# A hybrid decoder layer on one core: the delta rule's output with value channels on partitions, and the inverse's last levels paired across all heads

## The chip, the core and the metric

The kernel runs on one core of a Trainium2 chip. The core has five engines with queues of their own: TensorE (PE; its weight loads are listed as PEld), VectorE (DVE), ScalarE (ACT), GpSimd (POOL), and SyncE (SP), which here only issues DMAs. The metric is the device time of one execution in microseconds; the kernel before takes 1123.69 us (median of 3 runs, 1123.31 to 1124.84).

## The reference

One layer on 1024 tokens of width 1024 in float32. After an RMSNorm with shift and scale, one projection feeds two groups side by side: a gated linear recurrence (RG-LRU, 512 channels) and a gated delta rule (4 heads of width 128). Their normalized outputs go through one output projection; a squared-ReLU MLP of width 4096 and a final RMSNorm follow. The change lies in the delta rule, computed in chunks, and in the normalization of its output:

```python
u = triangular_solve(tmat, v_beta);  w = triangular_solve(tmat, k_beta * exp(g))
attn = where(causal, einsum('bhnid,bhnjd->bhnij', q, k) * decay, 0.0)
...
def step(state, inp):
    v_new = u_n - einsum('bhck,bhkv->bhcv', w_n, state)
    o = einsum('bhck,bhkv->bhcv', qd_n, state) + einsum('bhij,bhjv->bhiv', attn_n, v_new)
    state = state * gl_n[..., None, None] + einsum('bhck,bhcv->bhkv', kt_n, v_new)
    return state, o
...
out_gdn = rms_norm(o, gdn_norm_w) * silu(z)          # per head and token
mix = concatenate([out_lru, out_gdn], axis=-1) @ w_out
```

q and k are normalized to unit length per head and token. A scale of q passes through o, so the kernel never scales q: it adds the sum of squares of q, with its factors, to the epsilon of o's norm.

## The kernel before

All matrices are held as tiles of 128 partitions by 1024 columns in a pool of 46 (`big`), with PSUM tiles of 512 columns (`ps`) and DRAM tiles for what must wait long (`z_d`, `k_d`, `dm_d`, `cat_d`). The large products (input projections, output projection, MLP) split each f32 operand into a high and a low f32r part and take three f32r products (`mm3`). The smaller ones, in the delta rule, are plain f32, which the profile shows as two PE instructions each; a transpose is one.

The program is first recorded as a list of operations (`Recorder`), each with its predecessors. It is then emitted in an order that stands in the file as packed data: `ORDER` is one permutation of all operations of all engines, and `SLOTS` gives each tile its buffer. Each engine and the DMA queue run their part of it in this order. All loads and nearly all stores go through SP's queue.

Because every operation is recorded by one helper, almost all rows of the profile show line 319; operations are told apart by the names of their tiles. `mms` records several matmuls as one operation (line 445).

The delta rule uses chunks of 128 tokens, 8 per head:

- `key(h)`: the convolved key `k_`, its transposes `ktok`, the products `kk`, and the matrices `LT` of all 32 chunks.
- `inverse()`: inverts the 32 unit triangular matrices. DVE inverts the 32x32 diagonal blocks of all chunks at once. Then PE joins them: `it` and `iy` join 32 to 64, `iw` and `iz` join 64 to 128. `iw(h)` reads partitions 0 to 63 and writes 64 to 127, `iz(h)` the other way round. ACT takes `iw` out of PSUM (`after_iw`) and `iz` reads the result; DVE takes `iz` out (`after_iz`). `mixed` alternates the matmuls of two blocks.
- `query(h)`: the convolved q with channels on partitions, its 8 transposes `qtok` for the sums of squares (`ssqq`), and the products `qk` with keys, multiplied by the decay (tile `dm`).
- `value(h)`: the values, transposed (`vtok`) to tokens on partitions (tile `nv`).
- `chain(h)`: the recurrence over the 8 chunks. Per chunk the products with the state and the inverse are `ch`, the output's two products `cho`:

```python
mm(po[:, os4], qT[:, ts_], S, True, False)
mm(po[:, os4], dm[:, ts_], vn, S is None, True)
```

The first operand after the output is the stationary one; the result has its columns on partitions. So o comes out with tokens on partitions. After the last chunk, o is squared (`zt`), summed over each row (`rso`), scaled by the inverse root (POOL's power, `rsqrt8`), transposed back with 8 PE transposes (`oT`), multiplied by the gate z (`zz`) and stored to `cat_d`, from where the output projection loads it (`gcm`, split into `gch` and `gcl`).

PE fills the gaps of the recurrence with the input projections (`q_p`, `v_p`, `lx_p`, `ly_p`). The output projection (`wg`, `wl`) and the MLP (`up...`, `dn`) follow. `mod_row` computes a row of factors, stores it to DRAM (`modd`) and loads it broadcast to all partitions (`g_bc`); its sum over partitions is a block of four matmuls into 32 partitions each (`g_r`).

## Time and profile before

| | |
|---|---|
| runs | 1123.31, 1123.69, 1124.84 us |
| span of the profiled execution, first to last instruction | 1121.3 us |
| busy: PE, PEld | 1111.5, 934.3 us |
| busy: DVE, ACT, POOL | 795.0, 622.0, 254.0 us |
| granted TensorE clock, mean | 0.998 |
| DMA | 234.00 MB, 209 GB/s on average |

The page gives of the profiled execution its span alone; the median of the runs is 2.4 us longer. In the rows, a group reads: line, engine, operation, out<-in by tile names, shape, count, then busy time and the mean length of one instruction. In the timeline, a row is start, length, engine, line, operation, and how many of one kind in sequence it stands for. PE's instructions overlap, so lengths add up to more than the time.

### The profile page before, as it was taken

The page shows a single profiled execution, that of the slowest core. Times are in us where ns is not written, and L with a number is a line of the kernel's source. Part 1 is how long each engine was busy: PE and PEld are TensorE (multiplying, and loading weights), DVE is VectorE, ACT ScalarE, POOL GpSimd, SP SyncE. Part 2 cuts the span into 40 slices and gives each one's busy share as a digit, 9 for nine tenths or more (in the row PEclk, how much of TensorE's full clock was granted, in tenths as well). Part 3 has the DMA queues.
Part 4 walks back from the last instruction along what each step waited for, and adds up shares of the span by engine and source line. Part 5 has one row for each costly group of instructions (what it writes and reads, how often), then busy time and mean ns, then how long its engine had stood idle before and what let it go on. Part 6 is the DMA issues. An engine that isn't in the chain of part 4 may idle for free.

```text
span 1121.3 us, 16537 instructions
## 1 busy us (share of the span) xinstructions
PE 1111.5 (99%) x6282; PEld 934.3 (83%) x6282; DVE 795.0 (71%) x1122; ACT 622.0 (55%) x967; POOL 254.0 (23%) x159
## 2 busy tenths in 40 slices
PE   9999999999999999999999999999999999999997
PEld 8889889999988877888888888788888888888886
DVE  4859886877878796888675767768664583874573
ACT  6549644466488973786555545556555333453352
POOL 1000100101011442100113123132400366903030
PEclk9999999999999999999999999999999999999999
DMA  9808716567632354321777586778999757954511
GB/s 348 257 20 293 252 38 184 162 195 244 209 96 95 114 206 128 135 85 58 262 239 285 189 277 234 257 243 310 401 397 396 257 183 256 335 173 179 206 75 75
DMA packets 127688, 234.00 MB, mean 209 GB/s; under 512 B 10933, under 2 KB 51450, under 8 KB 127610
## 3 DMA queue, kind: packets, MB, share of 16 engines
q1 hardware_dynamic: 127370, 232.73, 59.8%
q8 instruction: 49, 0.80, 0.3%
q10 hardware_dynamic: 240, 0.23, 0.1%
q14 instruction: 29, 0.24, 0.1%
HBM read 174.18 MB, written 58.74 MB: 208 GB/s over the span
## 4 chain that ended last, share of the span: by engine, by line
PE 93%; ACT 2%; DVE 1%; DMA 1%; issue 1%; SPq 1%; POOL 0%; POOLq 0%; ACTq 0%; DVEq 0%
PE dn L319 27%; PE upx L319 16%; PE upz L319 8%; PE q_p L319 4%; PE k_p L319 4%; PE v_p L319 4%; PE wg L319 4%; PE upy L319 4%; PE ly_p L319 4%; PE lx_p L319 4%; PE wl L319 3%; PE z_p L319 3%; PE ch L319 2%; PE cho L319 1%; DMA wk<-in_w_in_dram 1%
## 5 line engine op out<-in xcount | busy, mean ns | idle before, releaser
L319 PE MATMUL upx<-h2h,U 128*128 128x512 f32 x512 | 167.9, 395 | 0.0
L319 PEld LDWEIGHTS upx<-h2h,U 128*128 128x128 f32 x512 | 96.2, 188 | 22.5
L319 ACT ACTIVATE act<-act 128x512 f32<-128x512 f32 x112 | 70.8, 632 | 58.6 <-DVE act L319 56.5
L319 PE MATMUL upx<-h2l,U 128*128 128x512 f32 x256 | 101.1, 395 | 0.0
L319 POOL TENSOR_TENSOR wd<-wd,wd 128x512 f32<-128x512 f32 x32 | 46.4, 1452 | 236.2 <-DMA wd<-in_w_down_dram 143.5
L319 DVE TENSOR_TENSOR U<-wu,U 128x512 fp32r<-128x512 f32 x112 | 84.4, 776 | 20.7 <-ACT U L319 19.7
L319 PE MATMUL upz<-h2h,U 128*128 128x512 f32 x256 | 85.0, 394 | 0.0
L319 ACT CAST U<-wu 128x512 fp32r<-128x512 f32 x112 | 65.4, 617 | 19.9 <-DVE wu L319 18.2
L319 PEld LDWEIGHTS upx<-h2l,U 128*128 128x128 f32 x256 | 48.1, 188 | 11.8 <-issue 0.4
L319 PEld LDWEIGHTS upz<-h2h,U 128*128 128x128 f32 x256 | 48.1, 188 | 11.1
L319 ACT COPY ek<-upx 128x512 f32<-128x512 f32 x48 | 28.0, 583 | 51.3 <-PE upx L319 50.8
L319 PE MATMUL upz<-h2l,U 128*128 128x512 f32 x128 | 50.3, 393 | 0.0
L319 DVE TENSOR_TENSOR act<-upz,ek 128x512 f32<-128x512 f32 x32 | 22.1, 690 | 36.7 <-ACT ek L319 17.9
L319 POOL TENSOR_TENSOR R<-R,R_5o 128x1024 f32<-128x1024 f32 x8 | 24.5, 3077 | 80.6 <-DMA L<-aod 69.9
L319 PE MATMUL upy<-h2h,U 128*128 128x512 f32 x128 | 42.7, 395 | 0.0
L319 DVE TENSOR_TENSOR wu<-wu,wu 128x512 f32<-128x512 f32 x48 | 36.0, 760 | 2.1 <-DMA wu<-in_w_up_dram 1.9
L319 ACT ACT_TABLE_LOAD x24 | 30.8, 1283 | 2.5 <-issue 2.1
L319 POOL TENSOR_TENSOR ssq<-ssq,mhalf 128x1 f32<-128x1 f32 x16 | 12.8, 805 | 81.1 <-DVE ssq L319 81.0
L319 PE MATMUL q_p<-hh,q_wh 128*128 128x256 f32 (+2 forms) x96 | 30.1, 339 | 0.0
L319 PE MATMUL v_p<-hh,v_wh 128*128 128x256 f32 (+2 forms) x96 | 29.8, 340 | 0.0
L319 PE MATMUL q_p<-hl,q_wh 128*128 128x512 f32 (+2 forms) x96 | 29.7, 336 | 0.0
L319 PE MATMUL lx_p<-hh,lx_wh 128*128 128x256 f32 (+2 forms) x96 | 29.6, 333 | 0.0
(576 smaller groups left out, 3468.4 us busy)
## 6 DMA issues: line engine op xcount, KB each, us to landing
L<-aod SPq DMA_DIRECT2D x56, 512.0 KB, 5.1
R<-in_w_down_dram SPq DMA_DIRECT2D x40, 512.0 KB, 7.2
wu<-in_w_up_dram SPq DMA_DIRECT2D x32, 512.0 KB, 4.5
aod<-as SPq DMA_DIRECT2D x64, 256.0 KB, 5.6
wd<-in_w_down_dram SPq DMA_DIRECT2D x32, 512.0 KB, 5.2
aod<-act SPq DMA_DIRECT2D x48, 256.0 KB, 2.7
x<-in_x_dram SPq DMA_DIRECT2D x16, 512.0 KB, 3.6
sc_w<-in_w_mod_dram SPq DMA_DIRECT2D x16, 512.0 KB, 7.9
```

The lines of the kernel that those rows point to most:

```text
L319: op.fn(*[res(v) for v in op.a], **{n: res(v) for n, v in op.k.items()})
```

## The change

- `chain`: the output's products swap their operands, so that o comes out with value channels on partitions, which is the layout of z. Each half of o is squared out of PSUM by ACT (over `nv`, now called `os_`) and multiplied by z by DVE. The load of z moves ahead of the recurrence.
- `query`: the transposes `qtok` and the sums over their squares go. ACT squares q whole (`qs`).
- The norm: `os_ + qs` is summed over partitions by a block of four matmuls with `ones`, 32 output partitions each (`on{h}`). DVE turns 32x32 blocks so that the 1024 sums stand on partitions, POOL takes the power on 8 columns, DVE turns back, the factors are stored to DRAM (`on_d`) and loaded broadcast (`nb`), and DVE multiplies `zz` by them. The reduction, the scaling of `nv` and the transposes `oT` go.
- `inverse`: `iz(h - 1)` is mixed with `iw(h)` for every h, also across the middle: one `iw` alone, three mixed blocks, one `iz` alone.
- `ORDER` and `SLOTS` are new as a whole (packed data, left out), with all loads placed for eight SP transfers in flight.

```diff
@@ inverse
-        for g in (0, 2):
+        for h in range(NH + 1):
             for q0 in (0, 4):
-                mms(iw(g, q0))
-            after_iw(g)
-            for q0 in (0, 4):
-                mms(mixed(iw(g + 1, q0), iz(g, q0)))
-            after_iz(g)
-            after_iw(g + 1)
-            for q0 in (0, 4):
-                mms(iz(g + 1, q0))
-            after_iz(g + 1)
+                mms(mixed(iw(h, q0), iz(h - 1, q0)) if 0 < h < NH else iz(h - 1, q0) if h else iw(h, q0))
+            if h:
+                after_iz(h - 1)
+            if h < NH:
+                after_iw(h)
@@ query
+        qs = big(f"qs{h}")
+        A.activation(qs, qT, AF.Square, scale=math.sqrt(1.28e-4))
         for hf in range(2):
-            pq = ps(f"qtok{h}_{hf}")
-            for j in range(4):
-                t = hf * 4 + j
-                tr(pq[:, j * P:(j + 1) * P], qT[:, t * P:(t + 1) * P], ident)
-            sumsq(pq, ssqq[:, h * 8 + hf * 4:h * 8 + hf * 4 + 4])
@@ chain
+        os_ = nv
+        zz = big(f"zz{h}")
+        SP.dma_start(out=zz, in_=z_d[h])
...
-                mm(po[:, os4], qT[:, ts_], S, True, False)
-            mm(po[:, os4], dm[:, ts_], vn, S is None, True)
+                mm(po[:, os4], S, qT[:, ts_], True, False)
+            mm(po[:, os4], vn, dm[:, ts_], S is None, True)
             if t % 4 == 3:
-                A.copy(nv[:, (t - 3) * P:(t + 1) * P], po)
+                s4 = halves[t // 4]
+                A.activation(os_[:, s4], po, AF.Square, scale=P ** -0.5)
+                V.tensor_tensor(out=zz[:, s4], in0=po, in1=zz[:, s4], op=ALU.mult)
...
+        V.tensor_tensor(out=os_, in0=os_, in1=qs, op=ALU.add)
+        pr, rw = ps(f"on{h}"), big(f"on{h}_w")
+        mms([(pr[32 * j:32 * j + 32, 0:256], ones[:, 0:32], os_[:, 256 * j:256 * j + 256], True, True) for j in range(4)])
         hs = slice(h * 8, h * 8 + 8)
-        zt, zz = big(f"zt{h}"), big(f"zz{h}")
-        SP.dma_start(out=zz, in_=z_d[h])
-        A.activation(zt, nv, AF.Square)
-        V.tensor_reduce(out=rso[:, hs], in_=v3(zt), op=ALU.add, axis=AX.X)
-        V.tensor_scalar(ssqq[:, hs], ssqq[:, hs], 1.28e-4, 1.28e-10, op0=ALU.mult, op1=ALU.add)
-        V.scalar_tensor_tensor(out=rso[:, hs], in0=rso[:, hs], scalar=1.0 / P, in1=ssqq[:, hs], op0=ALU.mult, op1=ALU.add)
+        V.transpose(rw[:, 0:256], pr[:, 0:256])
+        V.tensor_scalar(rso[:, hs], rw[:, 0:256:32], 1.28e-10, None, op0=ALU.add)
         rsqrt8(rso[:, hs], rso[:, hs])
-        V.tensor_tensor(out=v3(nv), in0=v3(nv), in1=bc(rso[:, hs], P), op=ALU.mult)
-        for hf in range(2):
-            s = halves[hf]
-            po = ps(f"oT{h}_{hf}")
-            for j in range(4):
-                t = hf * 4 + j
-                tr(po[:, j * P:(j + 1) * P], nv[:, t * P:(t + 1) * P], ident)
-            V.tensor_tensor(out=zz[:, s], in0=po, in1=zz[:, s], op=ALU.mult)
+        V.transpose(rw[:, 256:512], bc(rso[:, hs], 32))
+        SP.dma_start(out=on_d[h:h + 1, :].rearrange("a (j n) -> (a j) n", j=4), in_=rw[0:P:32, 256:512])
+        nb = big(f"on{h}_b")
+        SP.dma_start(out=nb, in_=on_d[h:h + 1, :].to_broadcast([P, T]))
+        V.tensor_tensor(out=zz, in0=zz, in1=nb, op=ALU.mult)
```

## The prediction

> **What bounds the kernel now.** I read the page first, for the busy shares.

> ```profile
> span 1121.3 us, 16537 instructions
> ## 1 busy us (share of the span) xinstructions
> PE 1111.5 (99%) x6282; PEld 934.3 (83%) x6282; DVE 795.0 (71%) x1122; ACT 622.0 (55%) x967; POOL 254.0 (23%) x159
> ```

> TensorE is busy for 1111.5 of 1121.3 us and the next engine, VectorE, for 71%. A mean can hide stages with another limit, so the second view is the table of stretches. Its columns are the length, then the busy time of PE, of its weight loads, DVE, ACT and POOL, the granted clock, the DMA share and GB/s.

> ```profile
> core 0: us, PE busy (x) PEld busy (x) DVE busy (x) ACT busy (x) POOL busy (x), PEclk, DMA share, GB/s
> 0.00:28.00 28.00, 25.66 (x213) 22.81 (x214) 13.49 (x39) 18.96 (x31) 5.34 (x16) 1.00 0.98 348
> 196.00:224.00 28.00, 28.00 (x207) 26.16 (x207) 22.63 (x34) 11.60 (x19) 4.05 (x2) 1.00 0.51 164
> 336.00:364.00 28.00, 27.82 (x184) 24.66 (x183) 23.02 (x25) 24.77 (x31) 5.34 (x3) 1.00 0.28 95
> 560.00:1115.00 555.00, 554.59 (x2419) 449.22 (x2417) 362.99 (x399) 261.74 (x383) 167.97 (x95) 1.00 0.70 250
> 1115.00:1121.00 6.00, 0.00 (x0) 0.00 (x0) 1.61 (x5) 1.12 (x3) 0.55 (x1) 0.74 0.24 89
> ```

> PE lacks 2.3 us at the start and everything after 1115, which is the last normalization and store. In the delta-rule stretch (196 to 224) it has no idle time, in the one where head 3 ends 0.18 us, in the long MLP stretch 0.41 us of 555. At a granted clock of 1.00, time is the sum of what PE has to issue. So the change is worth what it takes out of PE's queue, minus what it puts in and what its new order leaves idle. A matmul's own length (270 ns and more) is no price, since matmuls overlap. The price is read from the distance between starts in PE's timeline.

> **The change part by part.** First, 64 transposes go: 8 of q and 8 of the output for each of 4 heads. One half of them as a group, and then a run of five and one alone in the timeline (columns: start, length, engine, what, count):

> ```profile
> L319 PE MATMUL oT<-ident,nv x32: 270/272/275, 220.7 to 358.3; 128*128 128x128 f32 x32
> ```

> ```profile
> 173.03 0.27 PE L319 MATMUL qtok<-ident,q0T 128*128 128x128 f32 x1
> 173.05 0.48 PE L319 MATMUL q_p<-hh,q_wl 128*128 128x256 f32 x2
> 173.37 0.40 PE L319 MATMUL q_p<-hh,q_wh 128*128 128x512 f32 x1
> ...
> 220.48 0.40 PE L319 MATMUL q_p<-hl,q_wh 128*128 128x512 f32 x1
> 220.72 0.71 PE L319 MATMUL oT<-ident,nv 128*128 128x128 f32 x5
> 221.19 0.47 PE L319 MATMUL q_p<-hl,q_wh 128*128 128x512 f32 x1
> 221.50 0.28 PE L319 MATMUL q_p<-hh,q_wl 128*128 128x258 f32 x1
> ```

> The first 512-column product holds PE for 220.72 - 220.48 = 0.24 us, so I count 0.24 for each such product and 0.12 for one of 256 columns. From 220.48 to 221.50 are 1.02 us with two 512-column products in them (0.48): five transposes cost 0.54 us, 0.108 each. The lone one looks like 0.02 (173.05 - 173.03), but the two products after it take 0.32 in place of 0.24, so it costs 0.10. The cost shows one matmul late. I take 0.108: 64 x 0.108 = 6.9 us out of the queue.

> [...]

> Second, each head gets one block that sums squares over the partitions: four f32 matmuls of 256 columns into 32 partitions each, eight instructions. The kernel has the same block already, for the g2 gate:

> ```profile
> 710.93 0.62 PE L319 MATMUL upx<-h2h,U 128*128 128x512 f32 x2
> 711.48 0.64 PE L445 MATMUL g_r<-g_acc,ones 128*32 128x256 f32 x8
> 712.05 0.51 PE L319 MATMUL upx<-h2l,U 128*128 128x512 f32 x1
> 712.39 0.63 PE L319 MATMUL upx<-h2h,U 128*128 128x512 f32 x2
> ```

> From 710.93 to 712.39 are 1.46 us with three 512-column products (0.72): 0.74 for the block, and 4 x 0.74 = 3.0 us into the queue.

> Third, the last two levels of the inverse. Before, there are six blocks of 64x64 products: twice iw alone, iw mixed with iz, iz alone. After, there are five: iw, three mixed, iz. One alone and one mixed (its 32 rows begin at 170.34 and are left out):

> ```profile
> 167.47 0.51 PE L319 MATMUL q_p<-hh,q_wh 128*128 128x256 f32 x2
> 167.90 1.14 PE L445 MATMUL iw<-aw,LT 64*64 64x64 f32 x16
> 168.97 0.63 PE L319 MATMUL q_p<-hl,q_wh 128*128 128x256 f32 x2
> 169.44 0.28 PE L319 MATMUL z_p<-hh,z_wh 128*128 128x256 f32 x1
> ...
> 170.01 0.40 PE L319 MATMUL q_p<-hh,q_wh 128*128 128x512 f32 x1
> ...
> 171.42 0.39 PE L319 MATMUL q_p<-hl,q_wh 128*128 128x256 f32 x1
> 171.65 0.39 PE L319 MATMUL qk<-q0T,kTl 128*128 128x128 f32 x2
> ```

> Alone: 169.44 - 167.47 = 1.97, less four 256-column products (0.48), is 1.49. Mixed: 171.65 - 170.01 = 1.64, less 0.36, is 1.28. Two alone go and one mixed comes: 2 x 1.49 - 1.28 = 1.7 us out.

> Fourth, the output products swap operands: S and vn become the weights, q and the decayed scores stream. All four are 128x128 f32, so count and size stay.

> ```profile
> 239.74 0.38 PE L319 MATMUL cho<-vn,q_dm 128*128 128x128 f32 x2
> 239.96 0.39 PE L319 MATMUL ch<-S,kTl 128*128 128x128 f32 x2
> ```

> One such product (two instructions) takes 0.22 us with its weight loads. I count no change. What is new is that a weight load now waits for S and vn, where before it could run ahead with q or dm. It can cost between nothing and, if all 60 stalled for half a product, 60 x 0.11 = 6.6 us. I take zero, because these products feed only the output, not the recurrence, and an order can set them after something else. A gain has no source here.

> Fifth, the work of the other engines. The rows of the old normalization, over four heads:

> ```profile
> L319 DVE TENSOR_REDUCE rso<-zt x4: 1212/1213/1220, 214.8 to 341.2; 128x8 f32<-128x1024 f32 x4
> L319 DVE SCALAR_TENSOR_TENSOR rso<-rso,ssqq x4: 166/166/1032, 216.0 to 343.5; 128x8 f32<-128x8 f32 x4
> L319 POOL TENSOR_TENSOR rso<-rso,mhalf x4: 1636/1638/1646, 216.3 to 344.7; 128x8 f32<-128x8 f32 x4
> L319 DVE TENSOR_TENSOR nv<-nv,rso x4: 1225/1226/1227, 217.9 to 346.3; 128x1024 f32<-128x1024 f32 x4
> ```

> and, from the groups by shape, a block transpose of DVE (2.07 us for the full width):

> ```profile
> L319 DVE STREAM_TRANSPOSE gg<-gc 128x1024 f32<-128x1024 f32 x1 | 2.1, 2069 | 0.0
> ```

> Per head DVE loses a reduction (1.21), a scaling (1.23), two half-width reductions of q's squares (an estimate of 0.6 each from the 1.21) and two short ones (0.17 each): 4.0 us. It gains an add and a multiply over 128x1024 (1.23 each), two 32x32-block transposes of a quarter of the width (2.07 / 4 = 0.52 each) and a short one: 3.7. ACT exchanges copies for squares, gets one full-width square for q and loses the one of the output and two half ones. POOL keeps its 1.64 us power. None of this is a term: DVE has 5 us free in each 28, and PE pays for none of it.

> Sixth, eight DMAs more on SP's queue: a store of 1024 factors per head and a load that broadcasts them. The broadcast waits for the store to land, and every load behind it in the queue waits too. The one such wait of today, from the queue's list of waits (total, times, longest), and then, from the tiles' own rows, when the heads' results are stored and when their halves are split for the output projection:

> ```profile
> SPq L319 <- DMA modd<-g_b: 6.6, 1, 6.6
> ```

> ```profile
> L319 SPq DMA_DIRECT2D catd<-zz x4: 326/326/441, 258.1 to 360.8; - x4
> ...
> L319 DVE TENSOR_TENSOR gcl<-gcm,gch x4: 668/684/1756, 373.8 to 394.0; 128x512 fp32r<-128x512 f32 x4
> ```

> SP stood 6.6 us behind that store, and PE lost nothing by it. The last head's result is stored at 360.8 and its last split for the output projection runs at 394.0, so a path that is longer by one or two such trips (at most 13 us) stays covered, and the transposes that stretched the old one up to 358.3 are gone. If that cover failed, the output projection would start late by the difference. I take zero between that and 6.6 us for each of four. The load of z is the same one, only issued ahead of the head's steps; with the squares of q, the factors and their broadcast it holds more tiles of the pool of 46, which shows, if at all, as a later load, the same price.

> Seventh, the whole order is new, and the diff cannot show it. Between start and tail the rows leave it almost nothing to win. At the start there is something: PE idles 2.3 us there and the chain of waits runs through a weight load.

> ```profile
> 9.20 8.37 DMA wk<-in_w_in_dram
> ```

> A load placed better or worse could move this by up to those 2.3 us either way; I take zero.

> Sum: -6.9 + 3.0 - 1.7 = -5.6 us on the profiled execution's 1121.3. Time saved early is not lost later, since the MLP stretch waits for no load (0.41 us idle of 555). The median of the runs, 1123.69, lies 2.4 us above the span, start and end of the execution, which nothing here touches: 1123.7 - 5.6 = 1118.1.

> **The rivals.** (a) The new order also shortens the start by the 2.3 us: 1115.8. For it: the DMA share there is 0.98 and one load sits on the chain. Against it: at that share another order moves the same bytes.

> (b) No change. Either the new order leaves PE 4 to 6 us idle in the delta-rule stretch, where it had none, or the transposes really cost only the 0.02 us to the next start: 64 x 0.02 = 1.3, and -1.3 + 3.0 - 1.7 is zero, 1123.7. Against the second stands the late cost counted above. [...] For the first speaks only that a longer chain per head gives an order more to misplace.

> (c) Slower: the broadcast of the norm factors holds SP as the store above did, 6.6 us, and the weights for the next projections are queued behind it. It decides from the point where PE sees more than 5.6 us of the four waits, that is 1.4 us each. If two of four reach PE in full: -5.6 + 13.2, 1131.3. Against it: SP stood as long before and PE did not notice.

> **How the numbers follow.** Forecast (1118.1) 0.56, (a) 0.15, (b) 0.18, (c) 0.11. A measurement of this kernel can tell about 0.2% from no change, 2.2 us. So faster is 0.56 + 0.15 = 0.71, same 0.18, slower 0.11. The low end takes the start's 2.3, the 0.6 us idle of the two late stretches, and the block at its drawn length of 0.64 (0.4 less in all) off 1118.1, and is rounded down for what starts read to 0.01 us leave open: 1114.0. The high end, 1125.5, takes in nearly all of (b) and leaves out (c).

> **What would show it.** After: no qtok or oT rows; PE's busy time near 1106; sixteen transposes' time gone from each head; a block of eight in each head at 0.7 us from its surroundings; three mixed blocks of the inverse; PE idle between 28 and 1110 still under 2 us. The prediction is wrong if PE shows idle time before cho (the swapped weights), before lx or ly products with a DMA named (the queue), or before the output projection (the longer path), or if the start moved by more than the sum.

## The result, and the profile after

The changed kernel takes 1151.92 us (median of 4 runs, 1151.52 to 1152.99), the kernel before 1123.64 beside it. The ratio is 1.0253, with a 95% interval of 1.0239 to 1.0266: 28.3 us slower, where 5.6 us faster was forecast and 1125.5 was the range's upper end.

The head of the page of the changed kernel:

```profile
span 1149.7 us, 16499 instructions
## 1 busy us (share of the span) xinstructions
PE 1119.0 (97%) x6250; PEld 930.8 (81%) x6250; DVE 779.6 (68%) x1118; ACT 623.1 (54%) x962; POOL 246.0 (21%) x159
```

PE lost 32 instructions, as counted (64 transposes out, 32 of the norm blocks in), and DVE 15 us of work. Yet PE is idle for 30.7 us, where it was for 9.8, and its busy time did not fall. The table of stretches shows where. Columns are those of the prediction's table; the stretches are set to the same stages.

```profile
core 0: us, PE busy (x) PEld busy (x) DVE busy (x) ACT busy (x) POOL busy (x), PEclk, DMA share, GB/s
0.00:28.00 28.00, 26.43 (x207) 23.31 (x208) 12.56 (x37) 18.09 (x28) 6.61 (x15) 1.00 0.98 350
205.00:233.00 28.00, 27.99 (x206) 25.28 (x204) 19.42 (x26) 9.33 (x14) 4.02 (x2) 1.00 0.62 199
400.00:428.00 28.00, 24.99 (x122) 19.72 (x122) 24.60 (x19) 20.45 (x29) 10.85 (x4) 1.00 0.92 335
460.00:488.00 28.00, 24.95 (x119) 19.54 (x118) 18.93 (x42) 17.54 (x36) 3.08 (x4) 1.00 0.14 57
488.00:516.00 28.00, 24.05 (x111) 17.66 (x109) 17.28 (x42) 18.32 (x39) 1.65 (x3) 0.94 0.32 113
591.00:1143.00 552.00, 549.99 (x2396) 444.52 (x2394) 344.58 (x392) 258.30 (x379) 160.52 (x95) 1.00 0.71 250
```

The start is no shorter (PE shows 0.8 us less idle time there, but 207 products in place of 213), and the delta rule's stretch is as full as before. The large gaps lie from 400 to 516 us, where the output projection ends and `h2` is transposed for the MLP, and where the edits touch no line. The list of PE's waits (total us, times, longest) names them:

```profile
engine line waited for: us in total, times, longest us
PE h2T L326 <- ACT h2r L326: 5.2, 4, 2.9
PE iw L452 <- issue: 4.6, 1, 4.6
PE gate L452 <- ACT ly_st L326: 3.0, 2, 2.6
PE h2T L326 <- DVE h2r L326: 2.5, 4, 1.1
PE ch L326 <- DVE r L326: 1.2, 1, 1.2
PE dn L326 <- DVE R_5l L326: 1.1, 1, 1.1
```

Of these rows only the fifth, `ch`, belongs to the recurrence. The largest single wait has no releaser at all ("issue"); it stands in the inverse. The 0.94 in the clock's column is a stretch of 3.41 us, from 493.2 to 496.6 us, at a granted clock of 0.50, right behind some of the `h2T` waits.

A busy share hides part of the loss, because overlapping products are drawn longer than the time they hold PE (0.39 to 0.40 us for one of 512 columns, 0.23 to 0.24 to the next start). From 28 to 100 us both kernels show 72.00 us of 72.00, but 508 products before and 494 after. So I also added up what the products need, from the distance of their starts where nothing waits (0.23 us for 512 columns, 0.12 for 256, 0.11 for a 128-column f32 one), and took it off the clock. This idle time, in us (figures of idle time by stage further down are made in the same way, and what a low clock costs is in them):

| stage (us, after) | before | after | more |
|---|---|---|---|
| start to 160: norm, key and z projections | 14.1 | 19.4 | 5.3 |
| 160 to 200: inverse | -1.2 | 5.2 | 6.4 |
| 200 to 400: delta rule | 4.0 | 7.9 | 3.9 |
| 400 to 460: output projection | 0.8 | 3.8 | 3.0 |
| 460 to 540: h2 and its transposes | 0.0 | 11.4 | 11.4 |
| MLP to 1100 | 1.3 | 3.1 | 1.8 |

Together 31.8 us more; 28.3 remain when some 3.5 us of saved work are taken off. (The -1.2 comes from small products that are shorter than counted.) Some 25 of the 31.8 us lie outside what the edits change: the first stage, a good half of the second (the pairing's share of it is measured below), and everything from 400 us.

### The profile page after: what moved, and what is told of

Same layout as the page of the kernel before. It is cut to its first block, busy times and chain, and to the rows that moved or that the text cites. A ratio compares the mean times of both kernels' runs of the same rounds, so it can differ in the third digit from the quotient of the medians.

```text
span 1149.7 us, 16499 instructions
## 1 busy us (share of the span) xinstructions
PE 1119.0 (97%) x6250; PEld 930.8 (81%) x6250; DVE 779.6 (68%) x1118; ACT 623.1 (54%) x962; POOL 246.0 (21%) x159
## 3 DMA queue, kind: packets, MB, share of 16 engines
q1 hardware_dynamic: 127978, 234.84, 59.2%
## 4 chain that ended last, share of the span: by engine, by line
PE 89%; ACT 4%; DVE 3%; DMA 2%; issue 1%; POOL 0%; POOLq 0%; ACTq 0%; DVEq 0%; SPq 0%
PE dn L326 25%; PE upx L326 15%; PE upz L326 8%; PE k_p L326 4%; PE upy L326 4%; PE q_p L326 4%; PE v_p L326 4%; PE ly_p L326 4%; PE lx_p L326 4%; PE wg L326 3%; PE z_p L326 3%; PE wl L326 3%; PE ch L326 2%; PE cho L326 1%; PE warm L326 1%
## 5 line engine op out<-in xcount | busy, mean ns | idle before, releaser
L326 POOL TENSOR_TENSOR R<-R,R_5o 128x1024 f32<-128x1024 f32 x8 | 20.6, 2576 | 93.1 <-DMA R<-in_w_down_dram 77.3
L326 DVE TENSOR_TENSOR wu<-wu,wu 128x512 f32<-128x512 f32 x48 | 39.9, 842 | 0.2
L326 ACT ACTIVATE vn<-ch,bcoef 128x128 f32<-128x128 f32 x32 | 11.7, 366 | 43.0 <-PE ch L326 43.0
L326 PE MATMUL z_p<-hh,z_wh 128*128 128x258 f32 (+2 forms) x96 | 29.5, 337 | 1.4 <-DVE ktail L326 0.6
L326 PE MATMUL v_p<-hh,v_wh 128*128 128x512 f32 (+2 forms) x96 | 29.9, 333 | 1.0 <-DVE q_st L326 1.0
L326 PE MATMUL q_p<-hh,q_wl 128*128 128x512 f32 (+2 forms) x96 | 30.6, 345 | 0.0
L326 PE MATMUL lx_p<-hh,lx_wl 128*128 128x258 f32 (+2 forms) x96 | 29.5, 334 | 0.0
```

Of the source, the lines that this page charges most:

```text
L326: op.fn(*[res(v) for v in op.a], **{n: res(v) for n, v in op.k.items()})
```

## The experiments

All of them are one of the two sources with another order (`ORDER`), other buffers (`SLOTS`), or a few lines changed. The kernel before ran beside each set, at 1123.5 to 1123.8 us.

**Mixing code and order: three that told little.** Theories: the order (O), the code (C), the placement of loads (L).

```diff
 e1: changed code; compute engines and loads in the order of before
 e2: code of before; order of the changed kernel
 e4: as e1, with the changed kernel's loads
-SLOTS
+SLOTS chosen anew (the buffer unused longest, in the order of emission)
```

> The changed program, with every operation that both programs share put back at its place in the order of before, on each engine; the new operations of the norm stand about where the old norm's stood, z's load ahead of the head's recurrence, and six loads are issued later because the new tiles take buffers. Theory O (the new order costs the time, the edits of the code save what was predicted): 1116 to 1121 us, some 5.6 below 1123.7. Theory C (the edits themselves cost it: swapped weights, longer norm, broadcasts): over 1135, with PE idle before cho, on or the output projection. Theory L (the places of the loads cost it): as O, because the loads are back too.

> The program of before, with every shared operation in the order of the changed one; the old norm's operations stand beside where the new norm's stood. Theory O: 1123.7 plus the 34 us that the new order loses (28.3 measured and 5.6 saved), 1152 to 1160 us. Theory C: 1121 to 1126. Theory L: as O.

> As the first of these (changed program, compute engines in the order of before), but the loads and stores stand in SP's queue in the sequence of the changed kernel, each beside the same PE work as there; seven loads had to be moved to find buffers. Theory L: most of the loss comes back, over 1140 us. Theory O with the compute engines' order as its place: within 4 us of the first one.

Measured: 1222.35 (ratio 1.0876, interval 1.0861 to 1.0891), 1238.3 (1.1030, 1.1011 to 1.1049) and 1256.27 (1.1189, 1.1167 to 1.1211). Every mixture is 70 us or more slower than both parents, so these say that order, buffers and code belong together, not which of them cost 28 us. The first one's list for SP shows how such a mixture fails: one store placed too early holds every load behind it.

```profile
SPq L311 <- DVE on_w L311: 72.8, 4, 41.7
```

From here on, an experiment gives up or exchanges the order of one stage at a time. Where its line says so, the buffers of all tiles are chosen anew, so another stage can still move with them.

**The late stages.** The changed code with the old order from the output projection on, and the reverse: the old code, unedited, with the new order from there on.

```diff
 e5: changed code
-ORDER, operations that start at 382 us or later in the kernel before: as in the changed kernel
+ORDER, operations that start at 382 us or later in the kernel before: as in the kernel before
+SLOTS chosen anew
 e15: code of the kernel before
-ORDER, operations that start at 394 us or later in the changed kernel: as in the kernel before
+ORDER, operations that start at 394 us or later in the changed kernel: as in the changed kernel
```

> The changed code and its order up to 394 us; from there (output projection, the transposes of h2, MLP), where the edits touch no line, every engine and the SP queue follow the order of the kernel before, and the tiles are given their buffers anew. Theory O (the order of the untouched stages makes TensorE wait): the waits that the changed kernel has from 400 to 540 us (about 15 us of idle TensorE) and about 3 us in the MLP go: 1134 us (1131 to 1138). Rival D (those waits are only delay handed down from the delta rule, so they come back under any order): over 1145 us.

Measured: 1134.68 (1133.40 to 1135.52), ratio 1.0096 (1.0079 to 1.0113): 17.2 us won. Not all of it is the late order: with the new buffers PE did not stop in the inverse either (busy for 10.00 of 10.00 us from 170 to 180), while a norm block at 351 us waited for 2.7. The cleaner pair is e9 and e10 below, which share code, buffers up to 340 us and order up to 382: 1149.38 and 1133.59, 15.8 us. The stretches of e5, for the two of above:

```profile
core 0: us, PE busy (x) PEld busy (x) DVE busy (x) ACT busy (x) POOL busy (x), PEclk, DMA share, GB/s
460.00:488.00 28.00, 27.73 (x142) 22.86 (x141) 22.92 (x56) 21.27 (x49) 3.19 (x4) 1.00 0.38 132
488.00:516.00 28.00, 28.00 (x135) 23.00 (x134) 23.19 (x45) 23.05 (x47) 2.47 (x3) 1.00 0.24 85
```

> The unchanged code of the kernel before in its own order up to the output projection (about 385 us); from there every engine and SP in the order of the changed kernel; its own buffers where they fit. Theory O (the new order of the untouched stages costs by itself the 17 us that giving it up won): 1141 us (1136 to 1143). Rival (those waits needed the edited stage's lateness): 1124 to 1128 us.

Measured: 1143.15 (1142.11 to 1144.97), ratio 1.0176 (1.0162 to 1.0190): 19.6 us lost without an edit, by the late order and the buffers that it needs. PE's waits in it begin with

```profile
PE h2T L325 <- ACT h2r L325: 5.2, 4, 2.9
PE h2T L325 <- DVE h2r L325: 2.5, 4, 1.1
```

the very rows of the changed kernel. So the late waits need neither the edits nor their lateness. What differs in the order can be read from the starts. Before, PE runs the 12 products of one output tile in a row, two such tiles for each 128 tokens, and then the 8 transposes of one tile of `h2`; each transposed half is copied out by ACT and DVE while the next 24 products run. In the new order the products of up to seven tiles alternate one by one, so tiles end late, and the transposes are strewn among them, mostly in ones, twos and threes; a transpose that finds its PSUM tile still being copied stops everything behind it (2.88 us in the last row below). First the kernel before, then the changed one:

```profile
464.41 0.39 PE L319 MATMUL wl<-wo3h,lch 128*128 128x512 f32 x1
464.64 1.03 PE L319 MATMUL h2T<-ident,h 128*128 128x128 f32 x8
465.43 0.48 PE L319 MATMUL wl<-wo3l,lch 128*128 128x512 f32 x1
```

```profile
465.56 0.39 PE L326 MATMUL wl<-wo0h,lcl 128*128 128x512 f32 x1
465.80 0.49 PE L326 MATMUL h2T<-ident,h 128*128 128x128 f32 x3
466.04 0.48 PE L326 MATMUL wg<-wo7h,gcl 128*128 128x512 f32 x1
...
467.30 0.39 PE L326 MATMUL wl<-wo0l,lch 128*128 128x512 f32 x1
470.57 0.33 PE L326 MATMUL h2T<-ident,h 128*128 128x128 f32 x1 [2.88 <-ACT h2r L326]
```

That this alternation is the reason was not tried by itself.

**The stop in the inverse.** It falls in the middle of one mixed block, between products of the same operands:

```profile
175.61 0.22 PE L452 MATMUL iw<-aw,LT 64*64 64x64 f32 x1
175.62 0.22 PE L452 MATMUL iz<-LT,aw 64*64 64x64 f32 x1
180.40 0.37 PE L452 MATMUL iw<-aw,LT 64*64 64x64 f32 x1 [4.57 <-issue]
```

The products after it are longer: 0.31 us in place of 0.22. Stretches of 2 us around it (same columns) show two things more: a granted clock of 0.50 behind the stop, and DMA engines that are full up to 178 us, while PE stands:

```profile
174.00:176.00 2.00, 1.84 (x113) 1.66 (x112) 1.50 (x2) 1.95 (x3) 0.00 (x0) 1.00 0.99 369
176.00:178.00 2.00, 0.00 (x0) 0.00 (x0) 1.96 (x2) 1.96 (x4) 0.00 (x0) 1.00 0.97 322
178.00:180.00 2.00, 0.00 (x0) 0.00 (x0) 1.07 (x2) 1.80 (x3) 0.00 (x0) 0.79 0.55 213
182.00:184.00 2.00, 2.00 (x9) 1.71 (x8) 0.28 (x1) 1.19 (x2) 0.00 (x0) 0.50 0.00 0
186.00:188.00 2.00, 2.00 (x16) 1.87 (x16) 0.69 (x1) 0.00 (x0) 0.00 (x0) 1.00 0.00 0
```

The new order packs `it`, `iy` and `iw` more densely: 338 small products in 10 us from 165.2 on, where the kernel before has at most 238 in any 10 us. PE's instructions come as packets of 16 KB, 49 in the whole kernel (one for each 255 of its 12,500 products and weight loads), on a DMA queue of their own (q8), which the profile counts on the same 16 engines as the loads (q8 0.3% of their time, q1 59.2%). So: is it the density (D), or packets that queue behind loads (F)? First, all buffers chosen anew, which shifts the loads a little and leaves every engine's order alone; then two loads moved away; then five held back behind the dense part.

```diff
 e6: changed code and order
-SLOTS
+SLOTS chosen anew (by the time at which a buffer comes free)
 e7: changed kernel, on SP:
-load v2_w, g1_b, kTl0, ktl2, g1_w2, ktl0 | g1_w4 ... sc2_w4
+load g1_b, kTl0, g1_w2, ktl0 | g1_w4 ... sc2_w4, v2_w, ktl2
 e9: changed kernel, on SP:
-load v2_w, g1_b, kTl0, ktl2, g1_w2, ktl0
+load kTl0, ktl0, g1_w2, v2_w, g1_b, ktl2   # ktl0 in the buffer that xtc leaves at 175 us
```

> The changed code and its order, instruction for instruction on every engine; only which of the 46 large, 8 PSUM and 13 inverse buffers a tile gets is chosen anew (the buffer that came free just long enough before). Theory B (tiles wait for buffers that are still read): 1146 us or less. Rival O (the order, not the buffers): 1150 to 1153 us.

> The changed kernel with its own buffers and compute order; on SP only, the loads of v2_w and ktl2 (512 KB each, first read at 216 and 262 us), which it issues at 169.7 and 172.4 us, go behind the load of sc2_w4 at 193 us. So three loads in place of five stand in the DMA engines when TensorE stops for 4.6 us at 175.8. Theory F (TensorE waits for its next instructions, which queue behind the loads, and then runs at half clock for about 6 us): the stop shrinks to under 1 us and the low clock goes: 1144 us (1143 to 1146). Rival D (360 small products in 10 us use up the instructions whatever the loads do): 1151 to 1153 us.

> The changed kernel with every compute engine's order as it is. On SP the load of kTl0 goes ahead of five others (ktl0, g1_w2, v2_w, g1_b, ktl2), and the first of these gets the buffer that TensorE leaves with the last of the dense small products (two later tiles exchange buffers for it), so that the five wait until about 175 us. In the changed kernel TensorE has started 2750 instructions (products and weight loads) at 173.4 us, when the runs without a stop get a 16 KB packet of instructions, but its packet starts at 178.2 us, as the loads are done. Theory F (that packet queues behind loads already issued): no stop at 175.8, no half clock from 179.5 to 186: 1151.9 - 4.6 - 2.8 = 1144.5 us (1143 to 1146.5). Rival D (the dense products alone outrun the supply of instructions): 1151 to 1153 us.

Measured: e6 1151.56 (ratio 1.0251, 1.0236 to 1.0267), e7 1153.68 (1.0264, 1.0249 to 1.0280), e9 1149.38 (1.0228, 1.0214 to 1.0242).

By its time e6 speaks for O. Its trace says more: the stop is gone (PE has no idle time from 170 to 180 us). A wait of 2.7 us of a norm block at 351 us, longer ones in the MLP and three more stretches of 3.41 us at a clock of 0.50 took its place, so that the total is the same by chance. With the same instructions in the same order, the difference at 175 us is one packet. The DMA queues between 171 and 177 us (packets, MB, share), first of the changed kernel, then of e6:

```profile
## 3 DMA queue, kind: packets, MB, share of 16 engines
q1 hardware_dynamic: 1390, 1.86, 96.2%
```

```profile
## 3 DMA queue, kind: packets, MB, share of 16 engines
q1 hardware_dynamic: 1082, 1.84, 93.2%
q8 instruction: 1, 0.02, 1.0%
```

In e6 PE has started 2750 instructions (products and weight loads) at 172.46 us, and the packet starts at 172.47. In the changed kernel it has them at 173.42, just after three loads were issued, and the packet starts at 178.17, when 408 of the 512 packets of 4 KB of these three and of the load ahead of them are done; PE stops after 2988, at 175.62. Being issued is not what counts: in e6, too, three loads had been issued, from 171.35 to 172.24, but their data began to move only at 172.31, just ahead of the packet; in the changed kernel it had been moving since 172.94. In e7, three loads of 512 KB still stood ahead: the packet started at 177.06, PE stopped at the same instruction, for 4.0 us in place of 4.6. In e9 it started at 174.07, behind the one load (`kTl0`) that was left ahead of it, and the stop shrank to 1.5:

```profile
PE iw L451 <- issue: 1.5, 1, 1.5
```

In all three with a stop (the changed kernel, e7, e9) PE stops behind the same instruction and goes on 1.3 to 1.4 us after the packet has landed. That speaks for F and against D: the same dense products run without a stop (e6), with a long or with a short one, as the packet comes. My expectation for e7 was wrong in its size, since three loads are nearly as good as five at holding a packet up. For e9 it was wrong in the total: idle PE fell by 4.8 us up to 200 us, but 2.6 of them were given back by 540. The waits for `ly_st` and `h2r` stayed, and between 400 and 540 us three stretches of 3.41 us at a clock of 0.50 followed such waits, where the changed kernel has one; e7 has three as well.

**The early stages.** The changed code with the old order up to the inverse and from the output projection on; and the old code with the new order of the compute engines up to 90 us.

```diff
 e8: changed code, SLOTS chosen anew
+ORDER up to 185 us and from 382 us on: as in the kernel before (loads near the seams moved)
 e16: code of the kernel before, SLOTS chosen anew
+ORDER of PE, DVE, ACT and POOL up to 90 us: as in the changed kernel
```

> The changed code; TensorE, VectorE, ScalarE and GpSimd follow the order of the kernel before up to the end of the inverses (185 us) and again from the output projection on (382 us), SP too but for loads moved near the seams; only the delta rule in between has the new order; buffers chosen anew. Theory O (the new order of stages the edits don't touch is the cost): the 18 us of the late stages and about 12 us up to 195 us go: 1121 us (1117 to 1126). Rival C (the edits themselves cost, through the norm's round trip): over 1133 us.

> The unchanged code of before; up to 90 us (norm and key projection, which no edit touches) TensorE, VectorE, ScalarE and GpSimd follow the order of the changed kernel, SP keeps its own; buffers chosen anew. At 80 us the changed kernel's TensorE has idled 3.2 us longer than before's. Theory O (that order makes it): 1126.7 us (1125.5 to 1128.5). Rival (SP's loads make it, or later stages take it back): within 1 us of 1123.5.

Measured: e8 1146.22 (1.0201, 1.0185 to 1.0216), e16 1132.72 (1.0082, 1.0065 to 1.0098). Between 20 and 180 us, where the old order was restored, e8's PE is idle for 3.4 us; it is 1.2 before and 10.4 in the changed kernel. So that part behaves as theory O has it. The rest missed: a small load that I had placed first on SP kept PE waiting 5.5 us at the start, and in the delta rule, with other buffers, it was idle 19.6 us against 7.9. e16 is 9 us slower for no edit at all, more than expected: 3.7 us of its idle time come between 80 and 160, as in the changed kernel (3.6), but 2.5 between 20 and 40, where the changed kernel has 0.6, probably because the new compute order met the old loads:

```profile
PE k_p L313 <- ACT wkh L313: 1.3, 1, 1.3
```

**The best order for the changed code.** e5 with its 2.7 us wait and the stop removed, and with the old start between 30 and 85 us.

```diff
 e10: changed code; ORDER from 382 us as in the kernel before; loads at 170 us as in e9
+SLOTS up to 340 us as in the changed kernel
 e11: as e10
+ORDER of PE, DVE, ACT and POOL from 30 to 85 us: as in the kernel before
```

> Order as before from 382 us on, as in the run that gave 1134.7 us, and the loads at 170 us held back as in the run above; up to 340 us the tiles keep the changed kernel's own buffers. In the run of 1134.7 us VectorE waited 4.2 us for a load of wo whose buffer was free late, and the norm block of head 3 with it 2.7 us, followed by 3.6 us at half clock (1.8 us). Theory W (these two were of my buffers' making): 1134.7 - 4.5 = 1130 us (1128 to 1132). Rival: the wait moves to the next load, 1134 to 1136 us.

> As the run above, and the compute engines follow the order of the kernel before between 30 and 85 us too (the key projection, which the edits don't touch; start of the new order's extra idle TensorE). Theory O: the 1.5 to 2.5 us that the new order loses there go: 1128 us (1126 to 1129.5). Rival: the seam gives them back: 1130 us or more.

Measured: e10 1133.59 (1.0087, 1.0073 to 1.0101), e11 1139.47 (1.0143, 1.0129 to 1.0157). In e10 the wait at 351 us is gone, 4.8 us of idle time between 340 and 360, but the loads held back now leave a stop of 1.6 us at 176 that e5 did not have, with 3.41 us at a clock of 0.50 behind it, and the total hardly moved. e11 gained at most 0.6 us of idle time up to 160 us and lost elsewhere: its stop in the inverse is longer, 2.8 us, and a norm block waits for 3.3 us again, each followed by the half clock. Its tiles have other buffers than those of e10, so it does not test the start alone. No version of the changed code that was run beats the kernel before.

**The pairing alone**, in the kernel before; first with buffers chosen anew, then with its own.

```diff
-        for g in (0, 2):
-            ... iw(g) | mixed(iw(g + 1), iz(g)) | iz(g + 1)
+        for h in range(NH + 1):
+            ... mms(mixed(iw(h, q0), iz(h - 1, q0)) if 0 < h < NH else iz(h - 1, q0) if h else iw(h, q0))
```

> The program of before and its order, with the inverse's pairing alone changed; the new mixed block stands where iz of head 1 stood. By the prediction's row-derived price 1.7 us less than before: 1122.0. If a block costs nothing because PE has something else to do: 1123.7, same. No theory of the order expects it slower.

> The kernel before with the inverses paired across heads alone; its order otherwise and its own buffers (two PSUM tiles of the inverse moved to free banks, one load moved behind the last reader of its buffer). The prediction's arithmetic: 1123.7 - 1.7 = 1122.0 us. The run with newly chosen buffers gave 1129.9 us; if that was the buffers, this is within 1 us of 1122; if the pairing itself makes a wait (block of head 2 due earlier), 1125 us or more.

Measured: 1129.92 (1.0059, 1.0047 to 1.0072), then 1126.11 (1.0024, 1.0015 to 1.0033). So 3.8 of the first 6.2 us were the buffers, and the pairing itself costs 2.6 us where 1.7 were to be saved. Its stretches over the inverse, where the kernel before has 20.00 of 20.00 twice:

```profile
160.00:180.00 20.00, 19.33 (x404) 16.60 (x397) 16.16 (x20) 14.42 (x23) 0.00 (x0) 1.00 0.40 134
180.00:200.00 20.00, 17.99 (x187) 16.47 (x186) 9.45 (x20) 5.94 (x11) 2.37 (x1) 1.00 0.65 200
```

PE idles 2.7 us here, in four waits: 0.7 in front of `iw` ("issue"), 1.1 in front of a `ch` product for DVE's `S`, 0.7 for ACT's `v_wh` and 0.2. In a mixed block, the products of head h wait for those of head h - 1 to have come back through ACT, so the four heads form one chain of five steps, where they were two chains of three. That this chain makes the four waits is the likely reason; no row names it, and it was not tried by itself.

**What the moved work is worth.** The transposes taken out of the kernel before; the norm blocks taken out of e10. e13 leaves out the sums of q's squares and the output's turn, e14 the norm's sums; what stands in their place has no meaning.

```diff
 e13
-                tr(pq[:, j * P:(j + 1) * P], qT[:, t * P:(t + 1) * P], ident)
-            sumsq(pq, ssqq[...])
+            sumsq(hT[0][0][:, halves[hf]].bitcast(F32), ssqq[...])
...
-                tr(po[:, j * P:(j + 1) * P], nv[:, t * P:(t + 1) * P], ident)
-            V.tensor_tensor(out=zz[:, s], in0=po, in1=zz[:, s], op=ALU.mult)
+            V.tensor_tensor(out=zz[:, s], in0=nv[:, s], in1=zz[:, s], op=ALU.mult)
 e14
-        mms([(pr[32 * j:32 * j + 32, 0:256], ones[:, 0:32], os_[...], True, True) for j in range(4)])
-        V.transpose(rw[:, 0:256], pr[:, 0:256])
+        V.transpose(rw[:, 0:256], bc(ones[:, 0:8], 32))
```

> The kernel before without its 64 transposes of q and of the output (qtok, oT); order and buffers unchanged. ScalarE squares a part of h in place of q's transposes, VectorE multiplies z by the output as it stands: same instructions, other operands, so the normalisation and the orientation of the gated output are left out. The prediction's first term: 1123.6 - 6.9 = 1116.7 us (1116 to 1118). Rival (waits of the delta chain take the place of the transposes, which ran while the chain's VectorE and ScalarE steps were under way): 1120 us or more.

> The run of 1133.6 us without the four norm blocks on TensorE: VectorE transposes a constant in their place, everything behind it (square root, broadcast through DRAM, multiply) stays, so the norm's sum is left out. The prediction's second term: 4 x 0.74 = 3.0 us, and the waits in front of them (0.5 us): 1130.1 us (1129 to 1131.5). Rival (a block fills time in which TensorE would wait for the next head): 1132.5 us or more.

Measured: e13 1119.36 (1118.77 to 1121.53; ratio 0.9967, 0.9955 to 0.9979), 4.1 us faster (2.4 to 5.1 by the interval) and not 6.9. e14 1132.26 (1.0079, 1.0066 to 1.0091), 1.3 us under e10, with intervals that overlap, so not clear of nothing. The head of e13's page, beside the 1111.5 of before:

```profile
span 1116.9 us, 16404 instructions
## 1 busy us (share of the span) xinstructions
PE 1107.2 (99%) x6218; PEld 927.7 (83%) x6218; DVE 792.7 (71%) x1122; ACT 621.5 (56%) x967; POOL 255.3 (23%) x159
```

PE's idle time is 9.7 us, as before (9.8), and its list names no new wait of more than 0.2 us; so for the most part the work was smaller than priced.

## Why the prediction was wrong

**The step that failed is the seventh**, the new order at zero, with only the start's 2.3 us as its bound. I read in the rows that the order left "almost nothing to win" and bounded the step by that, but a full PE bounds only the gain: a new order of 8,200 operations can lose anywhere. e15 is that step by itself in the late stages, +19.6 us without an edit; e16 in the early ones, +9 with its seam. Giving up the late order won 15.8 us between e9 and e10 (buffers behind 340 us differ too), more than half of the 28.3 us. The stop in the inverse is also of the order, since the time at which its loads move decides on it (e6, e9); of the 6.4 us of idle time in that stage 2.6 are the pairing, if it costs there what it costs in e12.

**First, transposes, -6.9.** The mechanism holds, the size did not: -4.1 (e13, 2.4 to 5.1). From one start to the next, over the whole kernel, `qtok` holds PE 2.81 us for 32 and `oT` 2.27 us for 32, 5.1 in all, 79 ns each. My 108 ns came from one run of five among f32r products.

**Second, the norm blocks, +3.0.** The block of head 2:

```profile
266.62 0.64 PE L452 MATMUL on<-nv,ones 128*32 128x256 f32 x8
267.19 0.33 PE L326 MATMUL vtok<-ident,v2T 128*128 128x128 f32 x1
```

holds PE for 267.19 - 266.62 = 0.57 us, 2.3 for four, and without them 1.3 were measured, not clear of nothing. So both large terms were too big, and their errors partly cancelled: -2.8 by e13 and e14, -3.9 forecast.

**Third, the pairing, -1.7: the wrong sign.** +2.6 (e12). The blocks were priced as if PE could always start them, and 2.7 us of waits stand around them in e12; the chain through ACT, their likely reason, was not drawn up.

**Fourth, the swapped operands, 0:** right. No wait in front of `cho` is listed, and from start to start it takes 87 ns a piece, against 90. **Fifth, the other engines, 0:** right as a term. The work was not: 0.3 us less per head was counted, and DVE's busy time fell by 15.4 (779.6 against 795.0). **Sixth, the extra DMAs, 0:** SP does stand behind the factors' stores,

```profile
SPq L326 <- DVE on_w L326: 24.9, 3, 11.1
```

as rival (c) had it, but no wait of PE's list names what they hold; whether the late load of `wo` behind the wait before 416 us is theirs was not tried.

By terms, the edits are worth about -4.1 + 1.3 + 2.6 = -0.2 us, each measured in another order, so not to be taken as a sum to 1 us. What stays open: e10, the best version, is 10 us slower than before with the late order undone. 5.6 us of extra idle time lie ahead of 160 us (the order, by e8 and e16) and 2.6 in the inverse. The rest is spread over the delta rule in waits of at most 1.2 us, and whether another order would remove those, or the longer path of each head and its two more tiles per head make them, the runs don't tell.

## What to carry to other kernels

Where a whole order is exchanged with the edit, treat the order as the largest part of the change: a profile in which the bound engine never waits says how good the old order is, and nothing about the new one. Give the risk a price of its own, perhaps from how much idle time the engine would have if it met each cross-engine step with no slack (no run here tried that). And test it by giving the new order to unedited code, stage by stage; a seam is clean where both orders have nearly the same operations behind it.

## What the runs showed of the hardware

```profile
350.00:360.00 10.00, 8.95 (x57) 7.29 (x58) 7.27 (x9) 7.02 (x12) 5.10 (x3) 0.83 0.30 106
```

- The choice of buffers alone, with code and order equal, moved the same kernel by 3.8 us (e3 against e12), and in e6 removed one stop and made another.
